# Cross-covariance attention: Grams over 64 partitions, norms of Q from squares, stores in rows of 4 KB

## The chip, the core and the metric

The kernel runs on one core of a Trainium2 chip. The core has five engines that run their own instruction streams and meet at semaphores: TensorE (PE; its weight loads are listed as PEld), VectorE (DVE), ScalarE (ACT), GpSimd (POOL) and SyncE (SP), which here only issues transfers. Sixteen DMA engines move data between the main memory and the on-chip memory. TensorE writes its results to a separate memory, PSUM. The metric is device time in microseconds: 128.52 for the kernel before, the median of three runs (128.44 to 128.66).

## What is computed

```python
batch, heads, seq, dim = 8, 12, 512, 64
Q_norm = Q / (np.linalg.norm(Q, axis=-2, keepdims=True) + 1e-10)
K_norm = K / (np.linalg.norm(K, axis=-2, keepdims=True) + 1e-10)
attn = np.einsum('bhnd,bhne->bhde', Q_norm, K_norm)
attn = np.exp(attn - np.max(attn, axis=-1, keepdims=True))
attn = attn / (np.sum(attn, axis=-1, keepdims=True) + 1e-10)
return np.einsum('bhnd,bhde->bhne', V, attn)
```

There are 96 heads. Each has Q, K and V of 512 x 64 in float32. The norms are taken over the 512 positions, so each of the 64 columns has one; the attention matrix is 64 x 64, and the output is V times it. Inputs are 37.75 MB, the output is 12.58 MB.

## The kernel before

A unit `u` is four heads; two units make a step `s` (12 of them, `r` is 0 or 1 in it), two steps a group `w` (6). A unit of Q or K lies in the on-chip memory with 32 partitions per head and 16 positions per partition, so each partition takes one row of 4 KB of a 512 KB load. V comes in rows of 8 KB.

Loads are issued by SP in `load_qk` and `load_v`, except that the first two loads of K are issued by ACT. The very last unit (`WIDE`) is loaded in another way (`Qw`, `Kw`, L183): a head then has 64 partitions with 8 positions each, in rows of 2 KB. Q, K tiles of a step have three buffers, V tiles three.

For a unit, `cast_qk` makes a bf16 tile `qkb` of Q and K side by side (VectorE), and `grams` multiplies it with itself: 16 positions times 4 heads are 64 matmuls over 32 partitions each, with 128 x 128 results that hold Q'Q, Q'K, K'Q and K'K of a head. For the last unit it is 32 matmuls over 64 partitions. The results of a step are one PSUM tile, `gram`, with one buffer of 8 KB per partition.

For a step, `squares` picks the diagonals of Q'Q and K'K out of `gram` with an identity (two VectorE instructions of 64 partitions x 512) and `sums` adds them up; `powers` makes the inverse norms with a logarithm and an exponential (ScalarE); `cross` copies K'Q out of PSUM; `scale_k` scales it (GpSimd); `scales_q` moves the scales of Q into place with two small copies (ScalarE); `logits` transposes on TensorE; `exps` applies the exponential with the scale of Q and sums up (ScalarE); `normalise` divides (VectorE) into a bf16 tile `ab` that is block diagonal: head h of both units of the step.

V is cast to bf16 by `cast_v` (GpSimd, late in the kernel also VectorE), transposed on TensorE by `vtrans` and copied out of PSUM by `vcopy` (ScalarE, late also VectorE). `outs` makes an output tile `po` (s, x): 4 positions times 2 heads, 8 matmuls with 64 columns each. `ocopy` copies it into `so` (s, i), which holds one pair of heads of both units, and `store` writes such a tile of 512 KB as 256 rows of 2 KB. One store, `FEW`, is cut into four transfers. There are 13 `so` buffers.

The order of all this is not written out. Class `Order` takes the pieces with a cost for each engine that may do them, with what each must wait for, and a rank per kind (`R`, `BIAS`, and `QK_PACE`, `V_FROM`, `V_PACE`, `ST_LAG` for transfers), and lists them once, when the kernel is built. Each engine then runs its list in that fixed order, and so does SP with the transfers, where a store that has to wait holds up the loads behind it. The DMA queue takes a limited number of transfers (`QUEUE`). The second load of K of step 1 and what is behind it are held back until the first casts (`HELD`, `UNTIL`).

Of the kernel before, what the change touches and what calls it, by code (L numbers as in the profile page):

```python
# [102 lines left out]
def kernel(  # L103
# [14 lines left out]
    WIDE = U - 1  # L118
# [13 lines left out]
    Qw = Q.rearrange("b h (p j) d -> (b h p j d)", j=J).rearrange("(u m p x) -> u p m x", m=2, p=128, x=J * D)  # L132
    Kw = K.rearrange("b h (p j) d -> (b h p j d)", j=J).rearrange("(u m p x) -> u p m x", m=2, p=128, x=J * D)

    Of = out.rearrange("b h n d -> (b h n d)").rearrange(
        "(w r e i p x) -> w e i p r x", r=2, e=2, i=2, p=128, x=J * D)
# [3 lines left out]
    NB = dict(qk=3, v=3, vb=2, qkb=2, vt=2, so=13, sm=2, ab=4)  # L140
# [4 lines left out]
    qkp = ctx.enter_context(tc.tile_pool(name="qkp", bufs=NB["qkb"]))  # L145
    vtp = ctx.enter_context(tc.tile_pool(name="vtp", bufs=NB["vt"]))
# [6 lines left out]
    ps_g = grams_only.enter_context(tc.tile_pool(name="ps_g", bufs=1, space=bass.MemoryType.PSUM))  # L153
# [8 lines left out]
    qk32, v32, vb, qkb, gram, scr, kq, n2, r8, kqs, rq, lg, ex, ab, vps, vt, po, so = ({} for _ in range(18))  # L162
# [9 lines left out]
    def load_qk(s, x, r):  # L172
# [7 lines left out]
        if (s, x) == (0, 1):  # L180
            nc.scalar.dma_start(out=qk32[s][:, x, r].rearrange("p t d -> p (t d)"), in_=Ku[w, e, :, r])
        elif 2 * s + (r or 0) >= WIDE:
            nc.sync.dma_start(out=qk32[s][:, x, r].rearrange("p (m j) d -> p m (j d)", m=2), in_=(Qw, Kw)[x][U - 1])  # L183
        elif r is None:
            nc.sync.dma_start(out=qk32[s][:, x].rearrange("p r t d -> p r (t d)"), in_=(Qu, Ku)[x][w, e])
        else:
            nc.sync.dma_start(out=qk32[s][:, x, r].rearrange("p t d -> p (t d)"), in_=(Qu, Ku)[x][w, e, :, r])
# [10 lines left out]
    def store(s, i):  # L198
        o = Of[s // 2, s % 2, i].rearrange("p r (j d) -> p r j d", d=D)
        if (s, i) == FEW:  # L200

            for a, b in ((0, 92), (92, 100), (100, 128)):
                nc.sync.dma_start(out=o[a:b, 0], in_=so[s, i][a:b, 0])
            nc.sync.dma_start(out=o[:, 1], in_=so[s, i][:, 1])
            return
        nc.sync.dma_start(out=o, in_=so[s, i])

    def cast_qk(u, x):
        s, r = divmod(u, 2)
        if x == 0:  # L210
            qkb[u] = qkp.tile([128, T, 2 * D], BF16, name="qkb")
        nc.vector.tensor_copy(qkb[u][:, :, x * D:(x + 1) * D], qk32[s][:, x, r])  # L212
# [7 lines left out]
    def grams(u):  # L220
# [3 lines left out]
        if r == 0:  # L224
            gram[s] = ps_g.tile([128, HU, 2, 2, 2 * D], F32, name="gram")
        for t in range(T if u < WIDE else J):
            for h in range(HU):
                if u < WIDE:
                    x = qkb[u][32 * h:32 * (h + 1), t, :]
                else:  # L230
                    x = qkb[u][64 * (h % 2):64 * (h % 2 + 1), J * (h // 2) + t, :]
                nc.tensor.matmul(gram[s][:, h, r, 0], x, x, start=(t == 0), stop=(t == (T if u < WIDE else J) - 1))  # L232

    def squares(s, n):

        if n == 0:
            scr[s] = small.tile([128, 2 * HU, D], F32, name="scr")
        half = (LO, HI)[n]
        nc.vector.scalar_tensor_tensor(  # L239
            out=scr[s][half], in0=gram[s][half, :, :, 0, half].rearrange("p h r d -> p (h r) d"), scalar=1e-20,  # L240
            in1=eye2[half, None, :].to_broadcast([D, 2 * HU, D]), op0=ALU.add, op1=ALU.mult,
        )

    def cross(eng, s):

        kq[s] = small.tile([128, 2 * HU, D], F32, name="kq")
        copy(eng, kq[s][HI], gram[s][HI, :, :, 0, LO].rearrange("p h r d -> p (h r) d"))

    def sums(s):
        n2[s] = small.tile([128, 2 * HU], F32, name="n2")  # L250
        nc.vector.tensor_reduce(out=n2[s], in_=scr[s], axis=mybir.AxisListType.X, op=ALU.add)  # L251
# [8 lines left out]
    def scale_k(eng, s):  # L260
        kqs[s] = small.tile([128, 2 * HU, D], F32, name="kqs")
        (nc.vector if eng == "DVE" else nc.gpsimd).tensor_tensor(  # L262
            out=kqs[s][HI], in0=kq[s][HI], in1=r8[s][HI, :, None].to_broadcast([D, 2 * HU, D]), op=ALU.mult,
        )

    def scales_q(s):

        rq[s] = small.tile([128, HU], F32, name="rq")
        nc.scalar.copy(rq[s][LO], r8[s][LO, 0::2])
        nc.scalar.copy(rq[s][HI], r8[s][LO, 1::2])  # L270

    def logits(s):
        l = lg[s] = ps_l.tile([128, HU, D], F32, name="lg")
        for h in range(HU):
            nc.tensor.transpose(l[:, h, :], kqs[s][HI, 2 * h:2 * h + 2].rearrange("p r d -> p (r d)"), eye2[HI])  # L275

    def exps(s):
        e = small.tile([128, HU, D], F32, name="ex")
        z = small.tile([128, HU], F32, name="esum")
        for h in range(HU):  # L280
            nc.scalar.activation(e[:, h, :], lg[s][:, h, :], AF.Exp, scale=rq[s][:, h:h + 1], accum_out=z[:, h:h + 1])  # L281
# [27 lines left out]
    def outs(s, x):  # L309
# [3 lines left out]
        for j in range(J // 2):  # L313
            for e in range(2):
                h = 2 * i + e
                x16 = slice(16 * (4 * half + h), 16 * (4 * half + h + 1))
                v = vt[w][:, k * (J // 2) + j, x16, :].rearrange("p x c -> p (x c)")
                nc.tensor.matmul(po[s, x][e * D:(e + 1) * D, j].rearrange("p r d -> p (r d)"), v, ab[s][:, h, :])  # L318

    def ocopy(eng, s, x):  # L320
        i, k = divmod(x, 2)
        if k == 0:
            so[s, i] = sop.tile([128, 2, J, D], F32, name="so")
        o = so[s, i][:, :, k * (J // 2):(k + 1) * (J // 2)].rearrange("p r j d -> p j r d")
# [3 lines left out]
    for i in range(2):  # L328
        const.tile([128, D // 4], F32, name=f"front{i}")
# [15 lines left out]

    abs_ = []
# [151 lines left out]
```

## Time and profile before

| | |
|---|---|
| median of three runs | 128.52 us |
| profiled execution, its own time | 128.35 us |
| its span, first to last instruction | 126.5 us |
| first and last DMA packet of a tensor | 1.75 us, 125.4 us into the span |
| DMA, moved | 50.64 MB at 400 GB/s over the span |
| packets of 2 KB, 4 KB, 8 KB | 6656, 6144, 1420 |
| busy: TensorE, VectorE, ScalarE, GpSimd | 78.9, 90.7, 72.5, 37.4 us |

The page of a profile cuts the span into 40 equal slices and shows the busy share of each engine in tenths, 9 being 90% or more, with the mean share of the 16 DMA engines and what they moved. Its list of groups gives, for one line of code and one shape, the engine, the operation, output and inputs (partitions x elements), how many there were, then the busy time, the mean duration of one in ns, and the idle time of the engine just before them with what ended most of it. A timeline gives the start, the duration, the engine, the line and the operation; in square brackets stands how long the engine had been idle and what ended that. A busy share above 1 for DMA means that packets of one engine overlap a little.

Where the chain of work that ended last was followed back from the end, the shares by engine are VectorE 34%, DMA 21%, TensorE 19%, ScalarE 10%.

### The profile page before, as it was taken

The page shows a single profiled execution, that of the slowest core. Times are in us where ns is not written, and L with a number is a line of the kernel's source. Part 1 is how long each engine was busy: PE and PEld are TensorE (multiplying, and loading weights), DVE is VectorE, ACT ScalarE, POOL GpSimd, SP SyncE. Part 2 cuts the span into 40 slices and gives each one's busy share as a digit, 9 for nine tenths or more (in the row PEclk, how much of TensorE's full clock was granted, in tenths as well). Part 3 has the DMA queues.
Part 4 walks back from the last instruction along what each step waited for, and adds up shares of the span by engine and source line. Part 5 has one row for each costly group of instructions (what it writes and reads, how often), then busy time and mean ns, then how long its engine had stood idle before and what let it go on. Part 6 is the DMA issues. An engine that isn't in the chain of part 4 may idle for free.

```text
span 126.5 us, 4885 instructions
## 1 busy us (share of the span) xinstructions
PE 78.9 (62%) x2128; PEld 64.2 (51%) x2128; DVE 90.7 (72%) x141; ACT 72.5 (57%) x220; POOL 37.4 (30%) x40
## 2 busy tenths in 40 slices
PE   0065393895964679958583999596676858473000
PEld 0054382784843568747372788484464746352000
DVE  3344749839899499899976798999999799740000
ACT  4000441539789077695883688694758969974000
POOL 4006307300745913043064303133363270300000
PEclk9999999999599555899998559959999999855555
DMA  3999999999999999999999999999999999999993
GB/s 129 408 434 411 427 413 421 413 434 408 430 417 418 409 422 417 398 414 425 422 417 412 418 419 421 416 423 423 401 415 411 402 401 407 400 407 408 405 382 149
DMA packets 15359, 50.64 MB, mean 400 GB/s; under 512 B 1130, under 2 KB 1130, under 8 KB 13930
## 3 DMA queue, kind: packets, MB, share of 16 engines
q1 hardware_dynamic: 15050, 49.29, 96.5%
q10 hardware_dynamic: 288, 1.05, 2.1%
q8 instruction: 16, 0.26, 0.7%
q14 instruction: 5, 0.04, 0.1%
HBM read 37.75 MB, written 12.58 MB: 398 GB/s over the span
## 4 chain that ended last, share of the span: by engine, by line
DVE 34%; DMA 21%; PE 19%; ACT 10%; issue 5%; POOL 2%; SPq 0%; DVEq 0%; ACTq 0%; POOLq 0%
DMA qk<-in_Q_dram 21%; DVE qkb L212 12%; PE gram L232 12%; DVE scr L239 7%; DVE ab L290 5%; ACT so L166 4%; PE po L318 3%; DVE vb L168 3%; ACT ex L281 3%; PE vps L301 3%; DVE n L251 3%; DVE vt L168 2%; ACT vt L166 2%; DVE so L168 1%; POOL kqs L262 1%
## 5 line engine op out<-in xcount | busy, mean ns | idle before, releaser
L232 PE MATMUL gram<-qkb 32*128 32x128 bf16 (+1 forms) x1504 | 36.9, 262 | 20.3 <-DVE qkb L212 7.1
L232 PEld LDWEIGHTS <-qkb 32*128 32x128 bf16 (+1 forms) x1504 | 31.0, 117 | 24.8 <-DVE qkb L212 8.9
L212 DVE CAST qkb<-qk 128x1024 bf16<-128x1024 f32 x48 | 35.3, 758 | 8.4 <-DMA qk<-in_Q_dram 6.8
L170 POOL TENSOR_SCALAR vb<-v 128x1024 bf16<-128x1024 f32 x19 | 22.0, 1169 | 43.9 <-DMA v<-in_V_dram 39.6
L166 ACT COPY so<-po 128x512 f32<-128x512 f32 x45 | 24.8, 593 | 6.6 <-PE po L318 6.5
L166 ACT COPY vt<-vps 128x1024 bf16<-128x1024 bf16 (+1 forms) x18 | 17.8, 987 | 16.5 <-PE vps L301 16.4
L318 PE MATMUL po<-ab,vt 128*64 128x128 bf16 x384 | 20.8, 252 | 5.1 <-ACT so L166 1.7
L301 PE MATMUL vps<-identb,vb 128*128 128x128 bf16 x192 | 18.4, 247 | 6.5 <-POOL vb L170 4.3
L262 POOL TENSOR_TENSOR kqs<-kq,r 64x512 f32<-64x512 f32 x12 | 14.1, 1171 | 26.7 <-ACT r L258 14.0
L239 DVE SCALAR_TENSOR_TENSOR scr<-gram,eye 64x512 f32<-64x512 f32 x24 | 16.5, 687 | 6.0 <-PE gram L232 5.8
L318 PEld LDWEIGHTS <-vt 128*64 128x64 bf16 x384 | 15.2, 127 | 9.4 <-issue 4.8
L301 PEld LDWEIGHTS <-vb 128*128 128x128 bf16 x192 | 13.5, 110 | 10.2 <-POOL vb L170 5.5
L281 ACT ACTIVATE ex<-lg,rq 128x64 f32<-128x64 f32 x48 | 14.5, 322 | 2.5 <-PE lg L275 2.3
L166 ACT COPY kq<-gram 64x512 f32<-64x512 f32 x12 | 7.0, 581 | 13.5 <-DVE scr L239 13.3
L290 DVE TENSOR_TENSOR ab<-ex,rinv 64x256 bf16<-64x256 f32 x24 | 13.4, 556 | 0.6
L281 ACT ACTIVATION_READ_ACCUMULATOR ex<-lg,rq 128x1 f32 x48 | 10.2, 213 | 0.0
L275 PE MATMUL lg<-eye,kqs 64*128 64x64 f32 x48 | 6.4, 258 | 4.3 <-POOL kqs L262 2.6
L251 DVE TENSOR_REDUCE n<-scr 128x8 f32<-128x512 f32 x12 | 8.1, 679 | 0.1
L168 DVE COPY vt<-vps 128x1024 bf16<-128x1024 bf16 (+1 forms) x8 | 7.9, 1020 | 0.1
L168 DVE CAST vb<-v 128x1024 bf16<-128x1024 f32 x5 | 7.0, 1399 | 1.3 <-DMA v<-in_V_dram 1.3
L275 PEld LDWEIGHTS lg<-eye,kqs 64*128 64x128 f32 x48 | 4.5, 156 | 6.1 <-POOL kqs L262 3.3
L287 DVE RECIPROCAL rinv<-esum 128x4 f32<-128x4 f32 x12 | 2.1, 172 | 3.4 <-ACT ex L281 3.2
(17 smaller groups left out, 16.0 us busy)
## 6 DMA issues: line engine op xcount, KB each, us to landing
out_dram<-so SPq DMA_DIRECT2D x23, 512.0 KB, 10.2
v<-in_V_dram SPq DMA_DIRECT2D x11, 1024.0 KB, 17.1
qk<-in_Q_dram SPq DMA_DIRECT2D x8, 1024.0 KB, 17.1
qk<-in_K_dram SPq DMA_DIRECT2D x8, 1024.0 KB, 17.9
qk<-in_Q_dram SPq DMA_DIRECT2D x8, 512.0 KB, 12.2
qk<-in_K_dram SPq DMA_DIRECT2D x6, 512.0 KB, 12.5
qk<-in_K_dram ACTq DMA_DIRECT2D x2, 512.0 KB
v<-in_V_dram SPq DMA_DIRECT2D x2, 512.0 KB
```

The costliest lines, as they stand in the source:

```text
L166: nc.scalar.copy(o, i)
L168: nc.vector.tensor_copy(o, i)
L170: nc.gpsimd.tensor_scalar(out=o, in0=i, scalar1=1.0, scalar2=0.0, op0=ALU.mult, op1=ALU.add)
L212: nc.vector.tensor_copy(qkb[u][:, :, x * D:(x + 1) * D], qk32[s][:, x, r])
L232: nc.tensor.matmul(gram[s][:, h, r, 0], x, x, start=(t == 0), stop=(t == (T if u < WIDE else J) - 1))
L239: nc.vector.scalar_tensor_tensor(out=scr[s][half], in0=gram[s][half, :, :, 0, half].rearrange("p h r d -> p (h r) d"), scalar=1e-20, in1=e ...
L251: nc.vector.tensor_reduce(out=n2[s], in_=scr[s], axis=mybir.AxisListType.X, op=ALU.add)
L262: (nc.vector if eng == "DVE" else nc.gpsimd).tensor_tensor(out=kqs[s][HI], in0=kq[s][HI], in1=r8[s][HI, :, None].to_broadcast([D, 2 * HU, ...
L281: nc.scalar.activation(e[:, h, :], lg[s][:, h, :], AF.Exp, scale=rq[s][:, h:h + 1], accum_out=z[:, h:h + 1])
L290: nc.vector.tensor_tensor(out=a[half, :, half], in0=e[half], in1=ri[half, :, None].to_broadcast([D, HU, D]), op=ALU.mult,)
L301: nc.tensor.transpose(ps[:, c, n, :], vb[w][:, J * c + j].rearrange("p r d -> p (r d)"), identb)
L318: nc.tensor.matmul(po[s, x][e * D:(e + 1) * D, j].rearrange("p r d -> p (r d)"), v, ab[s][:, h, :])
```

## The change

- Grams: all units now run over 64 partitions, two heads at a time. K's bf16 half of `qkb` is copied twice into a new tile `km`, once with the partitions of every second head set to zero and once with those of the others (`mask_k`, two VectorE instructions a unit, a per-partition factor from `pick`). `km` has 128 columns of weights against `qkb` (K and Q): 32 matmuls a unit with results K'K and K'Q of both heads. The `gram` tile is halved and has two buffers. The special last unit (`WIDE`, `Qw`, `Kw`) is gone, so its loads are rows of 4 KB.
- Norms of Q: ScalarE squares Q into a bf16 tile `q2` (`square_q`), and 8 matmuls a unit against `heads`, a tile with a column of ones per head, add up over the positions (`norms_q`). `halves_q` copies the result; two small VectorE instructions in `sums` add the two halves.
- `squares` and `cross` are one instruction each of 128 partitions x 256; `sums` reduces half as much; `scales_q` is gone; `logits` is 2 transposes of 128 columns instead of 4; `scale_k` has half the elements.
- Output: an `outs` matmul has 32 columns of V (every second one of the 64 before), and four heads fill a `po` tile: 16 matmuls instead of 8. The tile `so` (6 buffers of 8 KB per partition) holds a whole step; a store takes one unit in 128 rows of 4 KB and needs all four copies of the step. `FEW` still goes in pieces of 2 KB rows.
- The casts of Q may go to GpSimd, and new ranks, costs and paces give a new order. In the built program all 24 casts of Q are on GpSimd, as are 23 of the 24 casts of V; 8 + 3 of the copies of V's transposes and 13 of the 48 `so` copies are on VectorE (5 + 3 and 3 before). SP has four stores ahead of the last loads (five before).

```diff
-    NB = dict(qk=3, v=3, vb=2, qkb=2, vt=2, so=13, sm=2, ab=4)
+    NB = dict(qk=3, v=3, vb=2, qkb=2, vt=2, so=6, sm=2, ab=4, km=2, q2=2)
...
-    ps_g = grams_only.enter_context(tc.tile_pool(name="ps_g", bufs=1, space=bass.MemoryType.PSUM))
+    ps_g = grams_only.enter_context(tc.tile_pool(name="ps_g", bufs=2, space=bass.MemoryType.PSUM))
...
-        elif 2 * s + (r or 0) >= WIDE:
-            nc.sync.dma_start(out=qk32[s][:, x, r].rearrange("p (m j) d -> p m (j d)", m=2), in_=(Qw, Kw)[x][U - 1])
...
-    def store(s, i):
-        o = Of[s // 2, s % 2, i].rearrange("p r (j d) -> p r j d", d=D)
-        if (s, i) == FEW:
+    def store(s, r):
+        o, i = Of[s // 2, s % 2][:, r], so[s][:, r].rearrange("p t d -> p (t d)")
+        if (s, r) == FEW:
 
             for a, b in ((0, 92), (92, 100), (100, 128)):
-                nc.sync.dma_start(out=o[a:b, 0], in_=so[s, i][a:b, 0])
-            nc.sync.dma_start(out=o[:, 1], in_=so[s, i][:, 1])
+                nc.sync.dma_start(out=o[a:b, :J * D], in_=i[a:b, :J * D])
+            nc.sync.dma_start(out=o[:, J * D:], in_=i[:, J * D:])
             return
-        nc.sync.dma_start(out=o, in_=so[s, i])
+        nc.sync.dma_start(out=o, in_=i)
-    def cast_qk(u, x):
+    def cast_qk(eng, u, x):
         s, r = divmod(u, 2)
         if x == 0:
-            qkb[u] = qkp.tile([128, T, 2 * D], BF16, name="qkb")
-        nc.vector.tensor_copy(qkb[u][:, :, x * D:(x + 1) * D], qk32[s][:, x, r])
+            qkb[u] = qkp.tile([128, T, 2, D], BF16, name="qkb")
+        copy(eng, qkb[u][:, :, 1 - x], qk32[s][:, x, r])
+
+    def mask_k(u):
+
+        km[u] = kmp.tile([128, T, 2, D], BF16, name="km")
+        for a in range(2):
+            nc.vector.tensor_scalar(
+                out=km[u][:, :, a], in0=qkb[u][:, :, 0], scalar1=pick[:, a:a + 1], scalar2=None, op0=ALU.mult)
+
+    def square_q(u):
+        s, r = divmod(u, 2)
+        q2[u] = q2p.tile([128, T, D], BF16, name="q2")
+        nc.scalar.activation(q2[u], qk32[s][:, 0, r], AF.Square)
...
+            gram[s] = ps_g.tile([128, 4, 4 * D], F32, name="gram")
+        for t in range(T):
+            for g in range(2):
+                rows = slice(64 * g, 64 * (g + 1))
+                nc.tensor.matmul(
+                    gram[s][:, 2 * g + r, 0:2 * D], km[u][rows, t].rearrange("p a d -> p (a d)"), qkb[u][rows, t].rearrange("p x d -> p (x d)"),
+                    start=(t == 0), stop=(t == T - 1))
+
+    def norms_q(u):
+
+        s, r = divmod(u, 2)
+        for t in range(J):
+            nc.tensor.matmul(
+                gram[s][:, 0, 2 * D + HU * r:2 * D + HU * (r + 1)], q2[u][:, 2 * t:2 * t + 2].rearrange("p t d -> p (t d)"), heads,
+                start=(t == 0), stop=(t == J - 1))
...
+        nc.vector.scalar_tensor_tensor(
+            out=scr[s], in0=gram[s][:, :, 0:D], scalar=1e-20,
+            in1=eye2[:, None, :].to_broadcast([128, 4, D]), op0=ALU.add, op1=ALU.mult,
         )
...
+    def halves_q(s):
+
+        hq[s] = small.tile([128, 2 * HU], F32, name="hq")
+        nc.scalar.copy(hq[s], gram[s][:, 0, 2 * D:2 * D + 2 * HU])
...
+        nc.vector.tensor_reduce(out=n2[s][:, 0:HU], in_=scr[s], axis=mybir.AxisListType.X, op=ALU.add)
+        for r, (here, there) in enumerate(((LO, HI), (HI, LO))):
+            cols, psum = slice(HU * r, HU * (r + 1)), slice(2 * D + HU * r, 2 * D + HU * (r + 1))
+            nc.vector.scalar_tensor_tensor(
+                out=n2[s][here, HU:2 * HU], in0=gram[s][here, 0, psum], scalar=1e-20, in1=hq[s][there, cols],
+                op0=ALU.add, op1=ALU.add)
...
         for j in range(J // 2):
-            for e in range(2):
-                h = 2 * i + e
+            for h in range(HU):
                 x16 = slice(16 * (4 * half + h), 16 * (4 * half + h + 1))
-                v = vt[w][:, k * (J // 2) + j, x16, :].rearrange("p x c -> p (x c)")
-                nc.tensor.matmul(po[s, x][e * D:(e + 1) * D, j].rearrange("p r d -> p (r d)"), v, ab[s][:, h, :])
+                v = vt[w][:, k * (J // 2) + j, x16, i::2].rearrange("p x c -> p (x c)")
+                nc.tensor.matmul(po[s, x][32 * h:32 * (h + 1), j].rearrange("p r d -> p (r d)"), v, ab[s][:, h, :])
...
+    nc.gpsimd.memset(pick, 0.0)
+    nc.gpsimd.memset(heads, 0.0)
+    for h in range(HU):
+        nc.gpsimd.memset(pick[32 * h:32 * (h + 1), h % 2:h % 2 + 1], 1.0)
+        nc.gpsimd.memset(heads[32 * h:32 * (h + 1), h:h + 1], 1.0)
...
-    QK_PACE, V_FROM, V_PACE, ST_LAG = 0.631, 0.0377, 0.7486, 1.5133
+    QK_PACE, V_FROM, V_PACE, ST_LAG = 0.6289, 0.0310, 0.6890, 1.1107
...
-        piece(("cq", u, 0), {"DVE": 0.72}, [loaded(0, s, r), back("gr", u, NB["qkb"])], [back("cq", u, 1, 1)], R["cq"] + 0.01 * u, cast_qk, u, 0)
+        piece(("cq", u, 0), {"DVE": 0.72, "POOL": (1.15, BIAS["cq"])}, [loaded(0, s, r), back("gr", u, NB["qkb"])], [back("mk", u, 1)], R["cq"] + 0.01 * u, cast_qk, u, 0)
+        piece(("q2", u), {"ACT": 0.95}, [loaded(0, s, r), back("nq", u, NB["q2"])], [back("q2", u, 1)], R["q2"] + 0.01 * u, square_q, u)
...
-            piece(("st", s, i), {"DMA": X}, [("oc", s, 2 * i), ("oc", s, 2 * i + 1)], order, v_at(2 * s + i) + ST_LAG, store, s, i)
+            piece(("st", s, r), {"DMA": X - 0.032}, [("oc", s, x) for x in range(4)], order, v_at(2 * s + r) + ST_LAG, store, s, r)
```

## The prediction

> **What bounds the kernel now.** I read the slices of the page first, then its groups, then busy time and DMA rate by stretch, and last the timelines of the final 30 us.
>
> ```profile
> DVE  3344749839899499899976798999999799740000
> DMA  3999999999999999999999999999999999999993
> GB/s 129 408 434 411 427 413 421 413 434 408 430 417 418 409 422 417 398 414 425 422 417 412 418 419 421 416 423 423 401 415 411 402 401 407 400 407 408 405 382 149
> ```
>
> In 38 of 40 slices the DMA engines are 90% busy or more, and the three from 114 us on in which VectorE is idle look no different. So transfers set the time: 50.33 MB of tensors, first packet 1.75 us and last 125.4 us into a span of 126.5. VectorE is the second limit: full from about 32 to 108 us. By stretch (us; busy of PE, PE loads, VectorE, ScalarE, GpSimd with counts; clock; DMA share; GB/s):
>
> ```profile
> core 0: us, PE busy (x) PEld busy (x) DVE busy (x) ACT busy (x) POOL busy (x), PEclk, DMA share, GB/s
> 10.60:14.50 3.90, 0.62 (x24) 0.35 (x16) 3.10 (x5) 0.95 (x3) 2.06 (x2) 1.00 1.03 417
> 18.60:26.50 7.90, 5.62 (x144) 4.37 (x136) 6.55 (x10) 3.09 (x8) 3.38 (x3) 1.00 1.02 417
> ...
> 113.00:117.00 4.00, 1.78 (x28) 1.29 (x23) 0.00 (x0) 2.15 (x4) 0.00 (x0) 0.50 1.05 407
> 117.00:121.00 4.00, 0.00 (x0) 0.00 (x0) 0.00 (x0) 0.00 (x0) 0.00 (x0) 0.50 1.05 408
> ```
>
> Apart from an instruction fetch, the first two stretches hold loads in rows of 4 KB and the last two stores in rows of 2 KB. Both are saturated, and the 2 KB rows run 2.4% slower. The packet records agree in sign: the median packet of 2 KB lasts 84 ns, of 4 KB 159, of 8 KB 309, so two small ones cost 9 ns more than one of 4 KB; packets of one DMA engine overlap a little (share 1.05), so the rates show less.
>
> How far is the arithmetic ahead of the transfers at the end?
>
> ```profile
> 114.52 1.07 ACT L166 COPY so<-po 128x512 f32<-128x512 f32 x2 [0.24 <-PE po L318]
> ```
>
> ```profile
> 115.81 4.22 SPq L206 DMA_DIRECT2D out_dram<-so  x4
> ```
>
> The last copy ends at 115.6 us. The last four stores are issued from 115.81, the last at 119.66, one per 1.29 us: the pace at which the DMA queue empties, not that of the copies. At those issues 3.3 us of transfers are still queued (bytes issued less bytes moved). That is the cover for arithmetic that gets later.
>
> **The change, part by part.**
>
> Rows of 4 KB. 23 of 24 stores of 512 KB (all but the one cut up as FEW) and the two last loads of Q and K (L183) go from 2 KB to 4 KB rows. 524,288 B at 407 GB/s are 1.288 us, at 417 they are 1.257: 0.031 us each, and 25 of them 0.78 us, all on the path. A store in 4 KB rows is not in this trace. Bounds: 0, if such a store is no faster than today's; 1.8 us by the packet records (3,200 pairs, 9 ns, 16 engines). I take 0.8, by the rates, since they hold the overlap.
>
> VectorE, 90.7 us busy. Rows:
>
> ```profile
> L212 DVE CAST qkb<-qk 128x1024 bf16<-128x1024 f32 x48 | 35.3, 758 | 8.4 <-DMA qk<-in_Q_dram 6.8
> ...
> L170 POOL TENSOR_SCALAR vb<-v 128x1024 bf16<-128x1024 f32 x19 | 22.0, 1169 | 43.9 <-DMA v<-in_V_dram 39.6
> ...
> L239 DVE SCALAR_TENSOR_TENSOR scr<-gram,eye 64x512 f32<-64x512 f32 x24 | 16.5, 687 | 6.0 <-PE gram L232 5.8
> ...
> L251 DVE TENSOR_REDUCE n<-scr 128x8 f32<-128x512 f32 x12 | 8.1, 679 | 0.1
> ...
> L168 DVE CAST vb<-v 128x1024 bf16<-128x1024 f32 x5 | 7.0, 1399 | 1.3 <-DMA v<-in_V_dram 1.3
> ```
>
> Counts are those of the built program. Off VectorE: all 24 casts of Q go to GpSimd, 24 x 0.758 = 18.2; squares go from 24 of 512 elements to 12 of 256 (0.42, the 64x256 ab row), 16.5 - 5.0 = 11.5; reduces halve in elements, 8.1 - 4.9 = 3.2; four of five V casts leave, 5.6. Sum 38.5. Onto it: 24 small sums at 0.17 (the reciprocal's row), 4.1; three more vt copies at 1.22, 3.7; ten more so copies at 0.69, 6.9; and 48 masks of K, bf16 to bf16. No row has such a mask. Its ends are 0.17 (the smallest instruction) and 1.22 (VectorE's vt copy, 1024 elements from PSUM). Nearest is the undisturbed cast, 0.685 and one started every 0.61; a mask moves 4 bytes per element where that moves 6, so I take 0.41, 19.7 in all. The Trainium skill, VectorE: DVE Perf Modes, perf-mode tier table and errata table, puts a 2-byte one-source operation in SBUF at four elements a cycle, an estimate of 0.33 us here; no run here shows it yet, and by it the masks would be 15.7. Onto VectorE then 34.4, less 38.5: -4.1.
>
> The port. GpSimd does 24 + 23 casts and 12 smaller kqs where it did 19 + 12: 37.4 us go to about 64.
>
> ```profile
> 53.86 0.69 DVE L212 CAST qkb<-qk 128x1024 bf16<-128x1024 f32 x1
> ...
> 54.18 1.28 POOL L170 TENSOR_SCALAR vb<-v 128x1024 bf16<-128x1024 f32 x1 [3.37 <-DMA v<-in_V_dram]
> ...
> 54.47 1.54 DVE L168 CAST vb<-v 128x1024 bf16<-128x1024 f32 x1
> ```
>
> The cast that began while GpSimd worked took 1.54 instead of 0.69. Such excess is 2.4 us in the Q/K casts, 3.6 in the V casts and 3.3 in ab (24 at 0.56 instead of 0.42): 9.3 us beside 36 us of GpSimd casts and products. At 1.8 times that it is some 17 us, +7.4. VectorE ends at 90.7 - 4.1 + 7.4 = 94.0. Between its first cast at 5.3 us and its last instruction at 112.3 it is idle 17.4 us today; half of that, 8.7, covers the 3.3.
>
> ScalarE, 72.5: 24 squares of Q at 1.01 (the vt copy, also 1024 elements) and 12 small copies at 0.19, +26.5; gone are 24 rq copies (4.6), ten so (5.9) and three vt copies (3.0), and kq is halved in elements (some 2.5): +10.5, to 83. Its idle 54 us hide that.
>
> TensorE, 78.9. The last unit already has Grams over 64 partitions:
>
> ```profile
> 98.31 1.07 PE L232 MATMUL gram<-qkb 32*128 32x128 bf16 x64 [0.34 <-ACT kq L166]
> ...
> 99.89 1.07 PE L232 MATMUL gram<-qkb 64*128 64x128 bf16 x32
> ```
>
> Half as many matmuls, the same 1.07 us: Grams cost nothing more. Norms are 8 matmuls a unit, at most the 0.61 us of 8 transposes of V: 24 x 0.61 = 14.6. Outputs double to 16 matmuls of 32 columns per po tile: between nothing (four column groups at once where two were) and 0.4 us at the half clock of the tail (8 in 0.65, 16 in 1.06). I take 0.2, 48 times 9.6. TensorE is then near 103 of 126, under the transfers; on the tail eight po tiles come 1.6 us later.
>
> Order. A store now needs all four copies of its pair, so the last two are both due after the last copy. The built SP queue has four stores ahead of the last loads where it had five, so those loads land 1.3 us earlier. Together with the 1.6 the last copy stays at 115.9. The second-last store is due at 118.38 - 0.8 = 117.6 with 3.3 us queued, and a transfer starts 1.0 us after its issue (first issue 0.74, first packet 1.75): a last copy up to 117.6 + 3.3 - 1.0 = 119.9 costs nothing, and beyond that each us costs one. K's and Q's buffers add no wait before that: from 20 to 90 us the queue holds 8 to 16 us of transfers. The new memsets of GpSimd at the start lie under the first load.
>
> Sum: 0.8 us off the path, the rest hidden. The profiled execution took 128.35 with a span of 126.5; it would be 127.55. The median of the runs is 128.52, 0.17 above, so **127.7 us**.
>
> **The rivals.**
>
> No gain from longer rows. A store writes to HBM, and the 4 KB rate is a load's; then the time stays 128.5. For it: no 4 KB store was seen. Against: the few 2 KB loads have the same 84 ns as the stores, so the size and not the direction sets it. The Trainium skill, DMA: Bandwidth & Descriptors, Specifications, has line rate from 512 B per transfer on, by which 2 KB rows would lose nothing and the time be 128.5. By that rule, this trace disagrees: 407 against 417 GB/s.
>
> VectorE becomes the bound. If a mask costs what the cast does, 0.685, the 48 are 32.9, 13.2 more; VectorE goes to 107. Of the 16.5 above today 8.7 go into idle time and 7.8 move the tail: last copy 115.9 + 7.8 = 123.7, 3.8 past 119.9, and the time is 127.7 + 3.8 = **131.5**. It decides from 4.0 us of lag at the tail. For it: VectorE is already full for 76 us, its instructions run in a fixed order, and GpSimd holds the port longer. Against: half the bytes, and the mask's output is needed one unit at a time, with two Gram tiles instead of one. Milder lags give 128 to 131.
>
> All of the packet difference counts. Then 1.8 us go and the time is 126.7.
>
> **How the numbers follow.** Forecast (0.5 to 1.1 us gained) 0.52; the full packet gain 0.08; no gain 0.13; VectorE late 0.27. A measurement of this kernel tells 0.2%, 0.26 us, from no change. So faster 0.60, same 0.13, slower 0.27. The likeliest case alone spans 127.4 to 128.1. The range takes in the full packet gain below and the late VectorE at its price above: 126.7 to 131.5.
>
> **What would show it.** Right: DMA busy in every slice, 2 KB packets gone but for FEW, about 417 GB/s in the last 25 us, a last so copy before 119.9, stores issued at even steps of 1.26 us to the end. Mask rows near 0.41; VectorE near 94; Grams near 1.1 us a unit; GpSimd near 64. Wrong: a slice with DMA below 9 before the end, SP waiting for a copy while the queue runs dry, masks at 0.69 or beside long casts, or store rates still at 407.

## The result, and the profile after

The changed kernel takes 136.47 us (median of 4 runs, 136.28 to 137.42), the kernel before, beside it, 128.51 (128.44 to 128.66): ratio 1.063, 95% interval 1.058 to 1.068. The prediction said 127.7, with a range of 126.7 to 131.5. The ratios here and below leave out every run that took over 1.5% more than the fastest of its kernel (one of e4's four, three of e11's four, three of e14's twelve); the medians hold all runs. The profiled execution has a span of 134.7 us, against 126.5.

From the page after, the slices of VectorE and DMA (40 of 3.37 us each) and the rate:

```profile
DVE  3383999963999899969999999999899999896000
DMA  4999999999999999999999999999999996074793
GB/s 119 410 427 417 432 420 421 413 428 417 422 416 420 427 413 424 410 424 423 412 427 415 427 416 421 424 411 417 418 407 417 411 417 249 2 296 174 235 415 135
```

Up to about 111 us the transfers are as full as before. Then come five slices at 249, 2, 296, 174 and 235 GB/s. Against 417 these five lack 2.7 slices, 9.1 us; the whole time is 8.0 us longer. So the time was lost in one place, between 111 and 128 us; the kernel before stored at an even pace there. And VectorE, which was idle from 114 us on, is now full until about 123. By stretch (columns as in the prediction):

```profile
108.00:112.00 4.00, 2.42 (x56) 1.94 (x56) 4.00 (x7) 1.36 (x10) 2.26 (x2) 0.73 1.01 410
112.00:116.00 4.00, 3.68 (x62) 3.44 (x66) 3.86 (x10) 1.53 (x7) 0.61 (x1) 0.50 0.33 131
116.00:120.00 4.00, 3.23 (x88) 2.57 (x80) 3.44 (x9) 3.75 (x14) 0.57 (x1) 0.92 0.31 123
120.00:124.00 4.00, 2.09 (x82) 1.61 (x83) 3.45 (x8) 2.94 (x12) 0.04 (x1) 0.93 0.52 207
```

What SP's queue waited for from VectorE (total, times, longest), first in the kernel before, then in the changed one the two largest, and the last copy of the changed kernel in the timeline:

```profile
SPq L185 <- DVE qkb L212: 5.2, 4, 2.9
```

```profile
SPq L181 <- DVE qkb L166: 20.5, 6, 5.3
SPq L202 <- DVE so L166: 15.2, 3, 6.9
```

```profile
126.80 1.07 ACT L164 COPY so<-po 128x512 f32<-128x512 f32 x2 [0.22 <-PE po L335]
```

Stores wait for VectorE's copies 15.2 us, loads for its casts of K 20.5. Such a wait costs time only where the DMA queue then runs dry, as it does here from 111 us on (e10, below, has 14.1 us of waits for casts of K and loses nothing). The last copy ends at 127.9, not at 115.9. The groups in which VectorE and GpSimd work between tiles of SBUF, the on-chip memory (busy, mean ns of one, idle before):

```profile
L168 POOL TENSOR_SCALAR qkb<-qk 128x1024 bf16<-128x1024 f32 x24 | 27.6, 1152 | 17.3 <-issue 4.7
L214 DVE TENSOR_SCALAR km<-qkb,pick 128x1024 bf16<-128x1024 bf16 x48 | 32.9, 726 | 0.6
L168 POOL TENSOR_SCALAR vb<-v 128x1024 bf16<-128x1024 f32 x23 | 27.7, 1218 | 5.1 <-DMA v<-in_V_dram 3.5
L166 DVE CAST qkb<-qk 128x1024 bf16<-128x1024 f32 x24 | 25.4, 1059 | 4.4 <-DMA qk<-in_K_dram 4.2
L308 DVE TENSOR_TENSOR ab<-ex,rinv 64x256 bf16<-64x256 f32 x24 | 15.9, 662 | 0.6
```

A cast of K has a mean of 1059 ns, where the Q/K casts before had 758; a mask 726, an ab product 662. VectorE is busy 107.8 us, GpSimd 64.7, ScalarE 80.2, TensorE 83.8. Taking for each of the three VectorE groups what its records last beyond the tenth percentile of the group, the excess is 9.1 us in the casts, 12.1 in the masks, 5.9 in ab: 27.1. The same measure gives 8.3 for the kernel before (casts of Q, K and V, and ab): 1.7 times the GpSimd time comes with 3.3 times the excess.

### The profile page after: what moved, and what is told of

It is laid out like the page before. It is cut to its first block, busy times and chain, and to the rows that moved or that the text cites. A ratio compares the mean times of both kernels' runs of the same rounds, so it can differ in the third digit from the quotient of the medians.

```text
span 134.7 us, 4632 instructions
## 1 busy us (share of the span) xinstructions
PE 83.8 (62%) x1944; PEld 69.5 (52%) x1944; DVE 107.8 (80%) x186; ACT 80.2 (60%) x219; POOL 64.7 (48%) x78
## 4 chain that ended last, share of the span: by engine, by line
DVE 26%; DMA 23%; PE 17%; issue 13%; ACT 7%; POOL 7%; SPq 1%; POOLq 1%; ACTq 0%; DVEq 0%
DMA qk<-in_K_dram 11%; DVE km L214 10%; PE gram L237 9%; DMA out_dram<-so 7%; DVE qkb L166 5%; DMA qk<-in_Q_dram 5%; DVE ab L308 4%; PE po L335 4%; POOL qkb L168 3%; POOL vb L168 3%; ACT so L164 3%; PE vps L319 2%; DVE vt L166 2%; ACT ex L299 2%; DVE scr L252 2%
## 5 line engine op out<-in xcount | busy, mean ns | idle before, releaser
L237 PE MATMUL gram<-qkb,km 64*128 64x128 bf16 x768 | 35.4, 262 | 19.2 <-DVE km L214 19.2
L237 PEld LDWEIGHTS <-km 64*128 64x128 bf16 x768 | 30.1, 118 | 22.6 <-DVE km L214 21.5
L168 POOL TENSOR_SCALAR qkb<-qk 128x1024 bf16<-128x1024 f32 x24 | 27.6, 1152 | 17.3 <-issue 4.7
L214 DVE TENSOR_SCALAR km<-qkb,pick 128x1024 bf16<-128x1024 bf16 x48 | 32.9, 726 | 0.6
L335 PE MATMUL po<-ab,vt 128*32 128x128 bf16 x768 | 21.6, 260 | 12.3 <-ACT so L164 8.5
L166 DVE CAST qkb<-qk 128x1024 bf16<-128x1024 f32 x24 | 25.4, 1059 | 4.4 <-DMA qk<-in_K_dram 4.2
L220 ACT ACTIVATE q<-qk 128x1024 bf16<-128x1024 f32 x24 | 25.3, 1061 | 4.6 <-DMA qk<-in_Q_dram 4.2
L335 PEld LDWEIGHTS <-vt 128*32 128x32 bf16 x768 | 15.5, 113 | 16.3 <-issue 13.3
L285 POOL TENSOR_TENSOR kqs<-kq,r 128x256 f32<-128x256 f32 x12 | 8.1, 679 | 32.1 <-ACT r L281 19.7
L299 ACT ACTIVATE ex<-lg,r 128x64 f32<-128x64 f32 x48 | 14.4, 315 | 4.9 <-PE lg L292 4.9
L299 ACT ACTIVATION_READ_ACCUMULATOR ex<-lg,r 128x1 f32 x48 | 9.9, 207 | 0.0
```

The source lines that it names most:

```text
L166: nc.vector.tensor_copy(o, i)
L168: nc.gpsimd.tensor_scalar(out=o, in0=i, scalar1=1.0, scalar2=0.0, op0=ALU.mult, op1=ALU.add)
L214: nc.vector.tensor_scalar(out=km[u][:, :, a], in0=qkb[u][:, :, 0], scalar1=pick[:, a:a + 1], scalar2=None, op0=ALU.mult)
L220: nc.scalar.activation(q2[u], qk32[s][:, 0, r], AF.Square)
L237: nc.tensor.matmul(gram[s][:, 2 * g + r, 0:2 * D], km[u][rows, t].rearrange("p a d -> p (a d)"), qkb[u][rows, t].rearrange("p x d -> p (x ...
L285: (nc.vector if eng == "DVE" else nc.gpsimd).tensor_tensor(out=kqs[s], in0=kq[s], in1=r8[s][:, 0:HU, None].to_broadcast([128, 4, D]), op=A ...
```

## The experiments

The theory after this reading: each GpSimd instruction holds up VectorE's work between SBUF tiles (the prediction calls this the port), and the 24 casts of Q that went to GpSimd (with four V casts) are most of the loss. Rivals: the masks alone are too much; the order is bad; the output part costs something that the prediction did not see. Times are medians; every ratio is against the kernel before on the same chip; busy times are in us.

**Who casts Q.** In e1 ScalarE casts Q, in e2 VectorE; everything else, the order too, stays.

```diff
-        copy(eng, qkb[u][:, :, 1 - x], qk32[s][:, x, r])
+        copy("ACT" if x == 0 else eng, qkb[u][:, :, 1 - x], qk32[s][:, x, r])
```

(e2: "DVE" in place of "ACT".)

> The changed kernel with one difference: the 24 casts of Q, at the same places of the order, are done by ScalarE instead of GpSimd. Port theory (GpSimd's casts hold VectorE up): VectorE's excess over undisturbed durations falls by half, from 30 us (masks 33 for 19, K casts 25 for 15, ab 16 for 10) to about 15, VectorE's busy time from 107.8 to 93 or less, a mask's mean from 0.73 to under 0.60, and the transfers no longer run dry for 10 us: 129 to 133 us, although ScalarE goes from 80 to about 105. Own-work theory (VectorE is late through its own masks and copies, whoever casts Q): mask mean stays above 0.68, VectorE above 103, time 135 to 140.

> The changed kernel with the 24 casts of Q on VectorE, at the same places of the order. Port theory: the excess falls as in the run with ScalarE, by about 15 us, and 24 casts of 0.61 come on, 14.6: VectorE stays near 107, time within 2 us of the changed kernel's 136.5, which says that the move to GpSimd gained VectorE nothing. Own-work theory: VectorE gets 15 to 18 us longer, over 120, and the time goes over 145.

| | time, us | ratio, interval | VectorE | GpSimd | mean mask, ns |
|---|---|---|---|---|---|
| changed kernel | 136.47 | 1.063 (1.058 to 1.068) | 107.8 | 64.7 | 726 |
| e1, Q by ScalarE | 131.26 | 1.024 (1.019 to 1.028) | 90.1 | 34.9 | 554 |
| e2, Q by VectorE | 136.57 | 1.063 (1.061 to 1.065) | 110.1 | 37.4 | 543 |

Off GpSimd, the casts give VectorE 17.7 us back and the kernel 5.2. In e1 the excess of the three groups is 9.0 us instead of 27.1. On VectorE, 24 more instructions make it only 2.3 us busier than in the changed kernel, and the time is the same: the move to GpSimd had gained next to nothing. But e1 still loses 2.4% with VectorE at 90.1, less than in the kernel before (90.7) and with ScalarE at 101.8, so VectorE's busy time is not all of it.

**The port by itself.** e8 leaves the attention out: it has instructions of VectorE and GpSimd alone and beside each other, on tiles of the kernel's sizes. One run. Its timeline, start and length of each series (L44 masks, L48 casts from f32, L52 copies out of PSUM, L56 GpSimd's casts):

> No attention is computed: two tiles are loaded and one is written. VectorE and GpSimd run in stages: 12 masks alone; 12 GpSimd casts alone; 24 masks beside 12 GpSimd casts; 24 casts of K beside 12; 24 so copies from PSUM beside 12; 24 masks beside 10 casts by ScalarE. Port theory: alone a mask takes 0.40 us from start to start and a GpSimd cast 1.04; beside each other they take turns, so that as long as both are busy one mask passes per GpSimd cast, every 1.4 to 1.5 us; casts of K the same, 1.7; copies from PSUM 0.69 as alone; beside ScalarE 0.40. Own-work theory: all as alone, or GpSimd alone gets slower.

```profile
6.32 4.84 DVE L44 TENSOR_SCALAR km<-kb,pick 128x1024 bf16<-128x1024 bf16 x12
...
12.07 12.14 POOL L56 TENSOR_SCALAR qb<-q 128x1024 bf16<-128x1024 f32 x12
...
24.81 18.94 DVE L44 TENSOR_SCALAR km<-kb,pick 128x1024 bf16<-128x1024 bf16 x24
24.94 14.18 POOL L56 TENSOR_SCALAR qb<-q 128x1024 bf16<-128x1024 f32 x12
...
44.41 24.61 DVE L48 CAST km<-k 128x1024 bf16<-128x1024 f32 x24
45.23 17.23 POOL L56 TENSOR_SCALAR qb<-q 128x1024 bf16<-128x1024 f32 x12
...
69.68 17.36 DVE L52 COPY so<-ps 128x512 f32<-128x512 f32 x24
69.93 12.14 POOL L56 TENSOR_SCALAR qb<-q 128x1024 bf16<-128x1024 f32 x12
...
87.82 9.59 DVE L44 TENSOR_SCALAR km<-kb,pick 128x1024 bf16<-128x1024 bf16 x24
```

A mask alone costs 4.84 / 12 = 0.40 us (beside ScalarE too: 9.59 / 24), GpSimd's cast 12.14 / 12 = 1.01. Together, one mask and one GpSimd cast alternate, a pair per 1.18 us (14.18 / 12), and 24 masks take 18.94 instead of 9.6: 9.3 / 12 = 0.78 us of VectorE for each GpSimd cast. Casts from f32 start every 0.61 us alone, 14.6 for 24; they take 24.61: 0.83 for each. The pairs, 1.18 and 1.44 us, came out below the 1.4 to 1.5 and 1.7 expected: they are 0.2 us shorter than their two instructions one after the other. Copies out of PSUM leave GpSimd at its 12.14. So the excess is a price per GpSimd cast that meets such work, nearly the same for the two VectorE instructions tried (0.40 and 0.61 us). The ab products and GpSimd's kqs products are not in e8. The Trainium skill, SBUF — State Buffer, section "SBUF: two separate sides", has it that GpSimd, and VectorE in an operation that uses two ports or has two SBUF inputs, take a shared pair of SBUF ports exclusively, for a whole instruction. The order of these series agrees, one instruction of each in turn; the 0.2 us by which a pair is shorter says that a part of each instruction lies outside its turn.

**The same without load on ScalarE.** e1 also put 25 us on ScalarE. In e9 GpSimd keeps its casts of Q at a sixteenth of their size; in e10 the masks are cut likewise. So e9 leaves out most of Q's bf16 copy, and e10 most of the masked K as well.

```diff
-            qkb[u] = qkp.tile([128, T, 2, D], BF16, name="qkb")
-        copy(eng, qkb[u][:, :, 1 - x], qk32[s][:, x, r])
+            qkb[u] = qkc[u % 2]
+        n = T if x else 1
+        copy(eng, qkb[u][:, :n, 1 - x], qk32[s][:, x, r, :n])
```

> The changed kernel with its order and engines, but each of the 24 casts of Q by GpSimd writes one of the 16 positions of a unit (128x64 elements instead of 128x1024) into tiles that are set up once and take turns; the other 15 positions of Q in bf16 are left out, so the crossed products hold little of Q. ScalarE gets nothing more, unlike in the run with Q cast by ScalarE. Port theory (what GpSimd's casts of Q hold of VectorE's port is most of the loss): VectorE near 90 (88 to 93), mask mean below 0.60 us, GpSimd near 40, time 129 to 131.3, that is like the run with ScalarE's casts or up to 2 us under it if ScalarE's 20 extra us cost that run something. Rival (the masks and the order by themselves, GpSimd's part small): VectorE over 98 and time over 134.

> As the run before this one, and the 48 masks also write one of 16 positions each; the rest of the masked K and of Q's bf16 copy is left out (and the constant added to the squares is larger, so that the logarithm stays defined on what is left). VectorE then has about 70 us of work, less than in the kernel before the change, and TensorE 3888 instructions and 15 fetches, fewer than before. What is left is the transfers with rows of 4 KB. If the gain that was predicted for the rows is there once arithmetic is out of the way: 127.4 to 128.1, ratio 0.991 to 0.997, and the DMA engines busy to the end. If rows give nothing: 128.4 to 128.7. If the order at the tail (stores that wait for four copies) costs by itself: over 128.8, with gaps in the last stores while VectorE is idle.

e9: 130.85 (129.99 to 131.88), ratio 1.021 (1.016 to 1.026), as e1, although ScalarE (80.4) has no more to do than in the changed kernel. GpSimd with 47.5 and VectorE with 94.4 are above what was expected: the small casts still take 0.34 us each, and setting up the two tiles 3.6. e10: 127.92 (127.73 to 128.19), ratio 0.9955 (0.994 to 0.997). VectorE's busy time is 90.7 there and not 70: a mask of a sixteenth still has 455 ns in the mean, against 241 in the median. Small instructions seem to wait for their turn too; by the measure above, e10's three groups still have 22.2 us of excess, so the port is far from empty in it. From the slices of e10 (3.16 us each):

```profile
DMA  3999999999999999999999999999999999999992
```

With the arithmetic early enough the rows of 4 KB give 0.58 us (0.4 to 0.8). From 98 to 121 us e10 moves 411 GB/s, the kernel before 405. The order of the stores costs nothing by itself.

**Halves of the change.** e3 is the kernel before with the output part alone (32 columns a matmul, 4 KB stores), order drawn anew with the old ranks; e5 the same with each engine's list as it was before, the two stores of a step at the place of the second. e4 is the changed kernel with the old output (64 columns, 2 KB).

```diff
-            for e in range(2):
-                h = 2 * i + e
+            for h in range(HU):
...
-                v = vt[w][:, k * (J // 2) + j, x16, :].rearrange("p x c -> p (x c)")
+                v = vt[w][:, k * (J // 2) + j, x16, i::2].rearrange("p x c -> p (x c)")
```

> The kernel before with the output part of the change alone: 32 columns an output matmul, tiles of a whole step, stores in rows of 4 KB. Grams, norms, ranks and paces are the old ones. If 4 KB stores run at the rate of 4 KB loads and the arithmetic stays ahead: DMA 0.72 us shorter, 127.6 to 128.0 us, ratio 0.993 to 0.997. If 4 KB stores are no faster: 128.4 to 128.6. If the store that waits for all four copies, or 16 matmuls a tile, are what made the changed kernel slow: over 129.5.

> The output part alone as in the run with rows only, but every engine keeps the list of the kernel before, instruction for instruction: 16 matmuls of 32 columns stand where 8 of 64 stood, and a step's first store goes to the place of its second. Order theory (it was the newly drawn order, with ranks made for other pieces, that cost 7.8 us there): 127.6 to 128.2 us, ratio 0.993 to 0.998, DMA without a hole. Output theory (the wait for four copies and 16 matmuls a tile cost it): over 130, with a hole of some us in the DMA rate after 100 us.

> The changed kernel with the old output: 64 columns a matmul, tiles of a pair of heads, stores in rows of 2 KB. Grams, norms, masks, GpSimd's casts of Q and the new ranks are kept. If VectorE and its port make the loss: VectorE 104 to 110 us busy, time 135 to 139. If the output part makes it: back under 131.

e3: 136.22 (1.059, 1.057 to 1.062); e5: 136.26 (1.060, 1.056 to 1.063). The rest of the change is not in them, and still they lose 7.8 us. I had not expected that of e3; that e5 repeats it takes the new order away as a reason. What it is shows in e5's timeline of TensorE:

```profile
68.59 1.07 PE L231 MATMUL gram<-qkb 32*128 32x128 bf16 x64
...
70.14 0.51 PE L231 MATMUL gram<-qkb 32*128 32x128 bf16 x23
73.79 1.35 PE L231 MATMUL gram<-qkb 32*128 32x128 bf16 x41 [3.13 <-issue]
```

TensorE stops 3.1 us after 23 of a unit's 64 Gram matmuls and goes on with the other 41. They read the same tile, so no data was missing; "issue" says that nothing the profile shows was waited for. What was missing are the instructions. e5 has eleven pauses of over 0.4 us without a wait, in the middle of one line's instructions (0.6 to 3.7 us, 23.6 in all). With matmuls and weight loads counted in order, every one of them comes 190 or 191 instructions past a multiple of 256; the one above comes after 2750, which is 10 times 256 and 190. The kernel before has six such pauses, all likewise placed, 7.2 us in all; the changed kernel has none. The queue named "instruction" brings packets of 16 KB; 4256 matmuls and weight loads over 16 of them (before), 5024 over 19 (e5), 3888 over 15 (after) and 3120 over 12 (e4) are 256 to a packet with a rest. When the packets began, in us:

```
before  ... 29.0 35.1 41.2 47.2 54.2 60.3 66.0 72.2 78.3 84.1 90.1 96.1 102.2 108.2
e5      ... 29.4 35.3 41.3 47.1 53.5 59.3 65.5 71.5 77.3 83.2 89.2  95.2 101.1 107.0 113.0 116.3 122.6
after   ... 29.0 39.2 46.8 52.8 62.9 68.7 77.2 85.1 91.9 99.2 106.3 113.5 118.9 125.3
```

In these three, while the DMA engines are full, packets never come closer than 5.7 us; in the first two they are mostly 6.0 apart. The kernel before is already at that pace from 29 us on, and has its last one at 108.2. Twice the output matmuls, 768 instructions more, are three more packets at the same pace: the sixteenth is at 107.0 in e5 as before, the last at 122.6. The changed kernel has 368 instructions fewer than the kernel before, packets mostly further apart than 6 us and no such pause: it isn't held by them. Nor is it the output part as such that costs: e10 and e14 (below) have it and lose nothing. Both kernels' class `Order` in fact holds this limit (`CHUNK, FETCH, FIRST = 256, 6.1, 190`) when it draws up the lists; the prediction did not use it. The Trainium skill, Runtime: NRT & Kernel Launch, section "Instruction fetch mechanics", has blocks of 256 instructions whose change is mostly hidden; on the size this trace agrees, on the hiding e5 differs, with pauses of up to 3.7 us.

e4: 133.6 (1.033, 1.029 to 1.037), VectorE 104.2: the time a little under what was expected, VectorE at the lower end. By the ratios, parts that cost 7.7 and 4.2 us alone come to 8.1 together, since the halved Grams pay for the output's instructions. Why the whole is some 4 us above e4 was not divided further (orders and the need of four copies differ).

**The order.** e6 is the changed kernel with its order drawn from durations of after's trace, ranks as they are:

```diff
...
-        piece(("cq", u, 1), {"DVE": 0.72}, [loaded(1, s, r)], [("cq", u, 0)], R["cq"] + 0.01 * u, cast_qk, u, 1)
-        piece(("mk", u), {"DVE": 0.70}, [("cq", u, 1), back("gr", u, NB["km"])], [("cq", u, 1)], R["mk"] + 0.01 * u, mask_k, u)
...
+        piece(("cq", u, 1), {"DVE": 1.06}, [loaded(1, s, r)], [("cq", u, 0)], R["cq"] + 0.01 * u, cast_qk, u, 1)
+        piece(("mk", u), {"DVE": 1.37}, [("cq", u, 1), back("gr", u, NB["km"])], [("cq", u, 1)], R["mk"] + 0.01 * u, mask_k, u)
...
-        piece(("nm", s), {"DVE": 1.12}, [("ex", s)] + [back("ou", s, NB["ab"], x) for x in range(4)], [], R["nm"] + 0.01 * s, normalise, s)
+        piece(("nm", s), {"DVE": 1.50}, [("ex", s)] + [back("ou", s, NB["ab"], x) for x in range(4)], [], R["nm"] + 0.01 * s, normalise, s)
...
```

> The changed kernel with its order drawn from the durations that its trace shows on VectorE and ScalarE (K casts 1.06 for 0.72, two masks 1.37 for 0.70, the division 1.50 for 1.12, squares 1.05 for 0.95, copies of V's transposes 1.22 and 1.03 for 1.42 and 1.31); ranks and paces as they are. VectorE then keeps 7 + 3 of the transposes' copies and 4 so copies instead of 8 + 3 and 13, and 19 casts of Q stay on GpSimd. If the loss is VectorE's total: VectorE about 100 us busy, 131 to 134. If no order can make up for it: 136 or more, unless the ranks fit the new costs worse.

e7 has the order of after, and ScalarE does the 13 `so` copies that VectorE had (`copy("ACT", o, po[s, x])`).

> The changed kernel, same order, the 13 so copies of VectorE done by ScalarE at the same places. They read PSUM, so GpSimd does not hold them up. If VectorE's total is what makes the stores late: 8.8 us come off it (99 of 107.8), and with about 3 us of that lost to ScalarE in the tail the time is 130 to 133. If only the port's waits matter, not VectorE's own work, it stays at 135.5 or more.

e6: 130.16 (1.015, 1.011 to 1.019), 6.3 us better with as much on the port: its trace has all 24 casts of Q on GpSimd (not 19), and the three groups still have 26 us of excess. But 4 of the `so` copies and 8 of the transposes' are VectorE's instead of 13 and 11, VectorE has 97.8, and the last cast of K ends at 104.8 us instead of 111.1. e7: 139.37 (1.083, 1.079 to 1.086), a miss; the number is the rival's (135.5 or more), but not for its reason: VectorE falls to 101.0, yet stores wait 16.4 us for ScalarE's copies, up to 9.8 at a time, and the last cast of K still ends at 109.6. ScalarE's list is in order too, and the copies stand in it behind work that waits. How much each of those waits adds was not divided.

**Can the whole change reach its gain?** Four kernels with all of the change and new orders; in the last three, ScalarE has some of the casts of Q and VectorE some more of V's:

```diff
-        piece(("cq", u, 0), {"DVE": 0.72, "POOL": (1.15, BIAS["cq"])}, [loaded(0, s, r), back("gr", u, NB["qkb"])], [back("mk", u, 1)], R["cq"] + 0.01 * u, cast_qk, u, 0)
+        piece(("cq", u, 0), {"ACT": (1.05, BIAS["ca"]), "POOL": (1.15, BIAS["cq"])}, [loaded(0, s, r), back("gr", u, NB["qkb"])], [back("mk", u, 1)], R["cq"] + 0.01 * u, cast_qk, u, 0)
```

with prices between those of before and after (mask piece 1.1, cast of K 0.9, `nm` 1.25) and new ranks. For e13 and e14 the ranks were sought on a model of the kernel with the times from start to start of these traces.

> The changed kernel in full, every cast of Q still by GpSimd; only the order and the sharing of copies are drawn anew, with the measured durations and with ranks sought on a model in which a VectorE instruction between two SBUF tiles and a GpSimd instruction take turns (20 so copies and 5 vt copies on VectorE, 28 and 21 on ScalarE). If the loss is VectorE's port excess where the order puts the work (the theory): between 127.9 (the transfers alone, as measured with the port emptied) and 130.2 (the earlier order by measured durations), VectorE 95 to 102. If the halved Grams with GpSimd's casts can't be placed at all beside the transfers: over 130.2.

> As the run before this one, but 7 of the 24 casts of Q are ScalarE's and 7 of V's VectorE's (another draw of ranks), so that GpSimd has 34 casts instead of 47. Theory: between 127.9 and 130, VectorE below the run before this one by some 6 us of excess less 4 us of V casts. If ScalarE (near 89 us of work) is what then holds the tail: over 130.2, with stores waiting for ScalarE's copies.

> The whole changed kernel. GpSimd has 15 casts of Q and 9 of V (ScalarE 9 of Q, VectorE 15 of V), in an order drawn with ranks sought on a replay in which VectorE and GpSimd take turns at SBUF. Theory (port and placing are all that keeps the change from its gain): 127.6 to 128.1, ratio 0.992 to 0.997, stores at even steps to the end, VectorE about 93. If the tail of the change costs by itself: 128.5 or more, with gaps between the last stores while VectorE and ScalarE are idle or wait for TensorE.

> As the run before this one with 14 casts of Q and 16 of V on GpSimd (30 in all) and another order. Theory: between the run before this one and the one with 34 casts, 127.7 to 128.5. If casts on GpSimd are not what decides: no order between the three, and 128.5 or more.

| | GpSimd's casts | time, us (lowest, highest) | ratio, interval | VectorE | ScalarE |
|---|---|---|---|---|---|
| e11 | 48 | 133.06 (130.17, 133.36) | none given | 105.2 | 81.0 |
| e12 | 34 | 128.77 (127.69, 129.05) | 1.000 (0.998 to 1.003) | 94.7 | 90.7 |
| e13 | 24 | 127.97 (127.62, 129.07) | 0.998 (0.996 to 1.000) | 88.5 | 96.0 |
| e14 | 31 | 127.82 (127.61, 130.53) | 0.995 (0.993 to 0.997) | 88.4 | 95.3 |

e11's only comparable run, the profiled one, took 130.17 us, the upper end of what was expected, but VectorE's 105.2 missed its range (95 to 102); with all casts of Q left on GpSimd at full size no order that was tried gets under 129.9. e14 beats the kernel before by 0.6 us and the changed one by 8.7; its median is 0.1 under e10's. e13's median lies in its range too, but its interval reaches 1. It had been expected that the number of casts ranks e13 and e14; it doesn't, and their intervals overlap. From the slices of e14, and two of its groups:

```profile
DMA  3999999999999999999999999999999999999993
GB/s 121 403 438 409 432 416 414 421 425 423 416 432 412 410 423 416 434 405 419 427 412 419 430 404 431 410 418 430 410 417 416 413 418 412 414 414 371 367 421 129
```

```profile
L214 DVE TENSOR_SCALAR km<-qkb,pick 128x1024 bf16<-128x1024 bf16 x48 | 25.7, 577 | 0.6
...
L166 DVE CAST qkb<-qk 128x1024 bf16<-128x1024 f32 x24 | 17.7, 738 | 7.7 <-DMA qk<-in_K_dram 7.6
```

DMA is 90% busy or more to the end, masks are back at 577 and casts of K at 738 ns, and the last cast of K ends at 100.8 us. All of the change is in it, so no part of it costs much by itself. Two slices near the end, at 371 and 367 GB/s, lack about 0.6 us against 411: what is left in the tail is of that size.

## Why the prediction was wrong

**Rows of 4 KB: right, a little over.** Taken 0.8 us; e10 and e14 gained 0.6. The sum had taken the loads' 417 GB/s for the stores; e10 shows 411 where the kernel before has 405. So the rival in which longer rows give nothing is out.

**The instructions: right, but for TensorE.** The mask taken at 0.41 is 0.40 from start to start; GpSimd near 64 is 64.7, ScalarE near 83 is 80.2, and a unit's Gram at the full clock still takes 1.07, with 32 matmuls instead of 64. On TensorE the norms took 8.7 us and the outputs 0.8 more, where 14.6 and 9.6 had been taken: 83.8 in place of 103.

**The port: the first step that failed.** "At 1.8 times that it is some 17 us, +7.4" scaled the excess of before with GpSimd's busy time. It is 27.1. A GpSimd cast takes 0.8 us from VectorE where it meets a mask or a cast (e8). VectorE now has 48 masks more and 28 casts fewer, 20 more such instructions in all, and less time for anything else, so more of GpSimd's 59 casts and products (31 before) meet one: 0.46 us for each in the mean, where 8.3 us over 31 are 0.27. The sum held even less than 17: the casts of Q and V had been taken off VectorE with their excess in them, some 4.6 us (24 at 0.758 and 4 at 1.40 for 0.685), and that was scaled all the same. Masks, casts of K and ab took 74.2 us where the sum had 57.6 (19.7, 17.1 and 13.4, and 7.4 for the port): 16.6 more, against 2.8 less in the rest, make VectorE 107.8 for 94.0. e1 takes the casts of Q off the port and e9 most of their work, and 5 of the 8 us go with that.

**The cover: the second step that failed, taken too large.** 17.1 us more on VectorE were to have 8.7 hidden in its idle time. The last copy came 12.0 us later than forecast (127.9 for 115.9), so 5.1 were. The threshold was about right: 8.0 us past 119.9 at one for one gives 127.7 + 8.0 = 135.7, measured 136.5. In the profiled executions last copies at 117.7 to 118.6 (e10, e12, e13, e14) go with 127.7 to 128.1 us, those at 120.7 to 129.2 (e6, e11, e9, e1, e7) with 0.7 to 1.9 us more than 127.55 and the lateness past 119.9. The rival in which VectorE becomes the bound thus had the place and, by chance, the busy time (107), but from a dear mask instead of the port, and its 131.5 was short by the same cover. e9 divides the miss: its VectorE, 94.4, is what had been forecast, and still its last copy ends at 121.6 and it takes 130.85, 3.2 us over the forecast. That part is not the size of the port's term but how little the order hides. e6 shows why the cover is small: the order prices a unit's two masks at 0.70 and a cast of K at 0.72, which took 1.45 and 1.06; with prices nearer to that, which also move copies to ScalarE, 6.3 us come back. The prediction took the order as given and moved only sums through it. The two remedies, e1 and e6, overlap: each alone leaves 1.5 to 2.4% of loss, and both in e14, with new ranks, leave none.

**TensorE: a limit that I left out.** "TensorE is then near 103 of 126, under the transfers" looked at busy time alone (83.8 in the end), not at the pace at which instructions arrive, though class `Order` has it. It is not what failed here: in the whole change the halved Grams happen to pay for it, which is luck; had the output part come alone, such a sum would have missed a loss of 7.8 us, with VectorE at 89.4.

**The order of loads and stores: right as to itself.** Neither the stores that need four copies nor the loads after four of them cost anything in e10, and hardly in e14.

## What to carry to other kernels

Price work that is moved to GpSimd on VectorE as well: count the GpSimd instructions that will meet VectorE work between SBUF tiles, and charge each about 0.8 us at the sizes of e8, instead of scaling an excess seen at lower load. Where an order is drawn from prices, compare each price with the trace before trusting what the order hides. Where transfers are saturated, count TensorE's instructions: here every 256, weight loads included, need about 6 us of time.

## What the runs showed of the hardware

The prediction did not reckon with the pace of the instruction packets: where TensorE was waiting for them (e3, e5) mostly 5.8 to 6.1 us apart under full DMA, although one lasts 0.9 to 1.0 us, and 3.3 or 3.5 at the end of e5 and e3, where stores leave gaps. The figure is no floor: one pair of e10 came 5.3 us apart under full DMA. Nor had it been expected that a small instruction may wait at the port as long as a large one: in e10 a mask of 128x64 has 241 ns in the median and 455 in the mean. That is read from one kernel, not tested by itself.
